# A two-layer transformer step on one core: the whole program ordered by the framework's timeline model

## The chip, the cores and the metric

The kernel runs on one core of a Trainium2 chip. Its time is device microseconds of one execution. The engines are TensorE (PE: matmuls, and PEld for their weight loads), VectorE (DVE), ScalarE (ACT), GpSimd (POOL) and SyncE (SP, which issues most of the loads). Each engine works through its own list of instructions in order and waits there for semaphores of the others.

## The reference

One inference step of a hybrid model, 1024 wide, for 128 context tokens and 512 latent tokens that go through the weights together. It has two layers, cut here to what the change touches:

```python
def trunk_layer(x, mods, gain1, gain2, w1, w2, mixer):
    shift1, scale1, gate1, shift2, scale2, gate2 = mods
    mix, aux = mixer(rms_norm(x, gain1) * (1 + scale1) + shift1)
    x = x + gate1 * mix
    h = rms_norm(x, gain2) * (1 + scale2) + shift2
    x = x + gate2 * (jnp.square(jax.nn.relu(h @ w1)) @ w2)
    return x, aux
```

`mods` is silu(c) times `w_mod`, 1024 by 6144 for each layer. The mixer of the first layer is softmax attention, with the keys and values of the context as further outputs. That of the second is a gated DeltaNet with eight heads: q, k, v and a gate z from a projection, a short convolution on q, k and v, and for each head a scan over chunks of 64 tokens in both directions. In a chunk a triangular matrix is inverted (`tinv`), and from chunk to chunk a 128x128 state is carried:

```python
v_new = u_i - w_i @ S
o = (q_i * jnp.exp(gc_i)[..., None]) @ S + qk_i @ v_new
S = S * jnp.exp(g_last)[..., None, None] + jnp.einsum('bhcd,bhce->bhde', k_i * ..., v_new)
```

The normalised and gated heads go through `w_out`. The final states are outputs too.

## The kernel before

Activations are held transposed, as 8 tiles of 128 features by 640 tokens. Each is split into a high and a low part, and each dense product is three products of such parts (`mm3`), 128x320 matmuls that follow each other. A weight block of 512 KB is loaded into one of three `raw` buffers by SP (L185), copied into its high part by ACT (L136) and subtracted to its low part by DVE or POOL (L133).

The program runs through the stages input and first norm (to about 48 us of the profile), attention (to 382), the first MLP (to 815), DeltaNet (to 1381) and the second MLP with the final norm.

Two things set the order of the work. The first is the order in which the code is written down. Where stages shall overlap, `weave` (L77) takes turns between generators, by weights. In `delta`, a round r weaves the projections and the convolution of head r (`dn_dense`), the decays of head r-1 (`dn_decay`), the inverse of head r-2 (`dn_inverse`) and the scan of head r-3 (`dn_scan`); rounds 6 and 7 also weave in the gates and outputs of heads 0 and 1 (`dn_z`, `dn_out`). Behind the rounds stands:

```python
        weave((self.dn_decay(n - 1), 20), (self.dn_inverse(n - 2), 4), (self.dn_scan(n - 3), 5))
        weave((self.dn_inverse(n - 1), 4), (self.dn_scan(n - 2), 5))
        drain(self.dn_scan(n - 1))
        ...
        weave((gated(left), 4 * len(left)), (mods(), MODW))
        self.first = self.prefetch(a["dn_w_out"][0], 0, [f * P for f in range(FT)])
        for i in range(DIRECT):
            self.load_act(i)
        drain(self.dn_out(n - 1))
```

`left` are the heads 2 to 7, and `mods()` computes two thirds of the second layer's `mods` (`modulate`, L362: 32x512 matmuls in four column strips of the array, 16 row blocks of `w_mod` in 32 loads). Heads 0 to 4 write their gated output to DRAM (`outd`, L1064) and `load_act` reloads it (L1123); heads 5 to 7 keep theirs.

The second is the framework's scheduler. It goes through the written program and gives each engine its list: where the next instruction in the written order isn't ready by its model of the machine, a later one that is ready may come first. So the z projections, which are written behind the last scan, already fill gaps of earlier scans in the order before. The scheduler's model is the default one of `tile.TileContext` (L1265).

A step of a scan (`step` in `dn_scan`, L994) is a chain: two matmuls with the state, `r` on DVE, a matmul `p1`, two copies on ACT, a matmul `p2` for the new state, which DVE adds up, and a matmul for the output. A scan has five pairs of steps, one of each direction, and a last pair for the context. The two states of a head are loaded by SP at its start (L1035).

Of the kernel before, what the change touches and what calls it, by code (L numbers as in the profile page):

```python
# [92 lines left out]
class Model:  # L93
# [76 lines left out]
            self.stt(y, t, 1.5, y, ALU.add, ALU.mult)  # L170
        return y

# [1 line left out]
    def raw(self, shape):  # L174
        return self.wp.tile(shape, F32, tag="raw", bufs=self.NRAW, name=self.nm("raw"))

# [46 lines left out]
    def prefetch(self, w, row0, cols):  # L223
        return [self.pair(w, row0, c) for c in cols[: self.NW // 2]]

# [1 line left out]
    def norm_acc(self, x, f, half):  # L227
        lo, hi = HALVES[half]
        if f == 0:
            acc = self.main("x", shape=[P, HALF])  # L230
            self.act(acc, x[f][:, lo:hi], AF.Square)
            self.sums[half] = [acc]
            return
        sq = self.half()
        self.act(sq, x[f][:, lo:hi], AF.Square)
        if f == FT - 1:
            self.sums[half].append(sq)
        else:
            acc = self.sums[half][0]
            self.tt(acc, acc, sq, ALU.add, self.nc.gpsimd)  # L240
# [66 lines left out]
                self.norm_acc(x, o, half)  # L307
        return sink

# [1 line left out]
    def setup(self):  # L311
        nc, a = self.nc, self.a
        self.ident = self.const([P, P])
# [147 lines left out]
            self.nc.sync.dma_start(out=x[f], in_=d[f])  # L461
        return x

# [1 line left out]
    def dec(self, dt=F32):  # L465
        return self.scr("dec", 3, [P, DEC], dt)

# [223 lines left out]
    def psum(self, name):  # L691
        return self.tc.tile_pool(name=name, bufs=1, space=bass.MemoryType.PSUM)

# [1 line left out]
    def mlp(self, l, h, x, first, mid):  # L695
        w1, w2 = self.a["mlp_w1"][l], self.a["mlp_w2"][l]
        NQ = DFF // D
        for q in range(NQ):
            acts = [(self.main("a", F32R), self.main("a", F32R)) for _ in range(FT)]

            def sink(o, half, ps):
                lo, hi = HALVES[half]
                r = self.half()
                self.act(r, ps, AF.Relu)
                t = self.half()
                self.stt(t, ps, 0.0, r, ALU.max, ALU.mult)
                self.split(t, acts[o][0][:, lo:hi], acts[o][1][:, lo:hi])

            yield from self.dense(w1, 0, [q * D + f * P for f in range(FT)], h, sink, first=first if q == 0 else None)
            yield from self.dense(w2, q * D, [f * P for f in range(FT)], acts, self.residual(x, l, 5, q == NQ - 1),  # L710
                                  last=GROUP if q == NQ - 1 else 1, mid=mid if q == NQ - 1 else None)

# [1 line left out]
    def vview(self, t, b, blk):  # L714
        base = t[:, 0, 0:1]
        pitch = list(base.ap[0])
        if blk is None:
            return bass.AP(base.tensor, base.offset, [pitch, [2 * b, T // (2 * b)], [T + b, 2], [1, b]])
        return bass.AP(base.tensor, base.offset + blk * P, [pitch, [2 * b, P // (2 * b)], [T + b, 2], [1, b]])
# [408 lines left out]
        self.acts[hd] = (self.main(tag, F32R), self.main(tag, F32R))  # L1128
        self.split(f, *self.acts[hd])

# [1 line left out]
    def run(self):  # L1132
        tc, nc, a = self.tc, self.nc, self.a
        pool = lambda name: tc.tile_pool(name=name, bufs=1)
# [134 lines left out]
```

## Time and profile before

| | us |
|---|---|
| median of 3 runs | 1922.67 |
| lowest and highest | 1917.06, 1923.22 |
| span of the profiled execution | 1910.3 |
| the median above that span | 12.4 |
| PE busy | 1800.1 (94%) |
| DVE busy | 1024.0 (54%) |
| ACT busy | 740.9 (39%) |
| POOL busy | 351.5 (18%) |

The profiled execution has its span as its own time; the runs of the table were timed apart from it. A line L146 is that of the helper for all matmuls and L133 and L139 are those of helpers on DVE, so groups are told apart by the tiles that they write and read. A weight or activation tile is named after its pool, as `scan`, `big`, `pd`, `blk`, `raw`. In the profile a matmul on fp32 data is two records, and one on the split parts one.

### The profile page before, as it was taken

To read this page: it belongs to the slowest core of one execution; us is meant where nothing else is said; L and a number is where in the kernel's file an instruction comes from. 1 tells how busy PE (TensorE), PEld (TensorE's weight loads), DVE (VectorE), ACT (ScalarE), POOL (GpSimd) and SP (SyncE) were. 2 spreads that over 40 slices of the span, in tenths; PEclk is the share of its full clock that TensorE was granted. 3 is DMA by queue.
4 is the path that set the end of the run, shared out by engine and by line. 5 is a ranking of instruction groups with operands and counts; after the bars stand their busy time and mean duration, and the time that the engine had idled before them with its cause. 6 is when DMAs were issued, how large, how long until landed. Compare 5 with 4: busy or idle time off the path is not lost.

```text
span 1910.3 us, 30501 instructions
## 1 busy us (share of the span) xinstructions
PE 1800.1 (94%) x11981; PEld 1667.6 (87%) x11981; DVE 1024.0 (54%) x2272; ACT 740.9 (39%) x1690; POOL 351.5 (18%) x379
## 2 busy tenths in 40 slices
PE   6998999999999999997899998899799999999998
PEld 2777877999999999997888888666799999999998
DVE  5546563534434434569888887744654434343442
ACT  2345542422313223356565546533433223131331
POOL 2343221300000000312333323321332000000002
PEclk9999999999999999998999999999898999999999
DMA  8641136245222222324122221456512222222211
GB/s 296 224 142 34 34 124 213 67 146 153 78 78 78 68 77 78 99 57 117 38 69 69 69 68 46 113 158 203 190 45 78 78 73 71 78 78 78 71 52 56
DMA packets 267669, 188.16 MB, mean 98 GB/s; under 512 B 40223, under 2 KB 242486, under 8 KB 267526
## 3 DMA queue, kind: packets, MB, share of 16 engines
q1 hardware_dynamic: 256032, 177.62, 31.7%
q10 hardware_dynamic: 10710, 6.83, 1.2%
q8 instruction: 94, 1.54, 0.3%
q0 software_dynamic: 784, 1.77, 0.2%
q14 instruction: 49, 0.40, 0.1%
HBM read 168.78 MB, written 14.79 MB: 96 GB/s over the span
## 4 chain that ended last, share of the span: by engine, by line
PE 75%; DVE 15%; DMA 5%; issue 2%; ACT 2%; POOL 0%; SPq 0%; ACTq 0%; POOLq 0%; DVEq 0%
PE dense L146 33%; PE pd L146 29%; PE scan L146 4%; DVE cv L139 2%; PE big L146 2%; PE mod L362 2%; PE pd L362 1%; DVE wide L133 1%; DMA wide<-gd 1%; DMA raw<-in_w_mod 1%; DVE w L133 1%; DVE ptmp L133 1%; DVE rst L133 1%; PE big L149 1%; PE S L146 1%
## 5 line engine op out<-in xcount | busy, mean ns | idle before, releaser
L146 PE MATMUL pd<-h,w 128*128 128x320 f32 x2016 | 358.7, 324 | 2.7 <-DVE a L133 2.4
L146 PE MATMUL dense<-a,wx 128*128 128x320 f32 x2238 | 337.0, 310 | 2.4 <-ACT wx L136 1.6
L146 PEld LDWEIGHTS dense<-a,wx 128*128 128x128 f32 x2238 | 329.7, 188 | 7.7 <-ACT wx L136 3.4
L146 PEld LDWEIGHTS pd<-h,w 128*128 128x128 f32 x2016 | 308.9, 194 | 15.7 <-issue 10.0
L136 ACT ACTIVATE wx<-raw 128x1024 fp32r<-128x1024 f32 x132 | 139.7, 1059 | 406.6 <-PE dense L146 220.6
L146 PE MATMUL dense<-h,wx 128*128 128x320 f32 x1776 | 265.1, 309 | 0.0
L146 PEld LDWEIGHTS dense<-h,wx 128*128 128x128 f32 x1776 | 261.6, 188 | 1.7 <-issue 1.7
L133 DVE TENSOR_TENSOR wx<-raw,wx 128x1024 fp32r<-128x1024 f32 x127 | 157.4, 1241 | 195.1 <-ACT wx L136 194.9
L133 POOL TENSOR_TENSOR x<-x,half 128x320 f32<-128x320 f32 x48 | 50.3, 1049 | 924.1 <-ACT half L136 889.8
L146 PE MATMUL pd<-a,wx 128*128 128x320 f32 x1284 | 194.3, 309 | 0.0
L146 PEld LDWEIGHTS pd<-a,wx 128*128 128x128 f32 x1284 | 189.6, 188 | 0.8 <-issue 0.8
L139 DVE SCALAR_TENSOR_TENSOR x<-dense,c,x 128x320 f32<-128x320 f32 (+2 forms) x152 | 61.8, 435 | 175.3 <-PE dense L146 175.2
L146 PE MATMUL pd<-h,wx 128*128 128x320 f32 x1008 | 151.8, 309 | 0.0
L146 PEld LDWEIGHTS pd<-h,wx 128*128 128x128 f32 x1008 | 148.8, 188 | 0.8 <-issue 0.8
L136 ACT ACTIVATE a<-half 128x320 fp32r<-128x320 f32 x128 | 60.1, 471 | 116.7 <-DVE half L139 116.7
L133 DVE TENSOR_TENSOR a<-half,a 128x320 fp32r<-128x320 f32 x128 | 62.8, 492 | 65.9 <-ACT a L136 65.6
L139 DVE SCALAR_TENSOR_TENSOR x<-pd,c,x 128x192 f32<-128x192 f32 (+2 forms) x88 | 36.0, 437 | 108.0 <-PE pd L146 108.0
L146 PE MATMUL scan<-blk,wide 128*128 128x128 f32 x288 | 64.9, 308 | 26.8 <-DVE blk L139 23.3
L146 PEld LDWEIGHTS scan<-blk,wide 128*128 128x128 f32 x288 | 44.6, 192 | 49.9 <-DVE blk L139 33.4
L139 DVE SCALAR_TENSOR_TENSOR cv<-cv,c,cv 128x644 f32<-128x644 f32 x84 | 84.3, 1004 | 2.0 <-ACT cv L136 0.9
L146 PE MATMUL big<-wide,a 128*128 128x128 f32 x480 | 71.9, 286 | 8.7 <-DVE wide L133 8.6
L136 ACT ACTIVATE w<-raw 128x1024 fp32r<-128x1024 f32 x54 | 57.0, 1060 | 45.4 <-PE pd L146 28.1
(276 smaller groups left out, 2529.9 us busy)
## 6 DMA issues: line engine op xcount, KB each, us to landing
raw<-in_mlp_w SPq DMA_DIRECT2D x128, 512.0 KB
raw<-in_w_mod SPq DMA_DIRECT2D x80, 512.0 KB
raw<-in_dn_w_in SPq DMA_DIRECT2D x32, 512.0 KB
raw<-in_attn_w_in SPq DMA_DIRECT2D x12, 512.0 KB
x<-xs SPq DMA_DIRECT2D x16, 320.0 KB
wide<-gd SPq DMA_DIRECT2D x16, 320.0 KB
h<-in_w_mod SPq DMA_DIRECT2D x16, 256.0 KB
a<-in_w_mod SPq DMA_DIRECT2D x16, 256.0 KB
```

What stands on the lines that cost most here:

```text
L133: (eng or self.nc.vector).tensor_tensor(out=out, in0=in0, in1=in1, op=op)
L136: self.nc.scalar.activation(out=out, in_=in_, func=func, **kw)
L139: self.nc.vector.scalar_tensor_tensor(out=out, in0=in0, scalar=s, in1=in1, op0=op0, op1=op1)
L146: self.nc.tensor.matmul(out, l, r, start=first, stop=last)
L149: self.nc.tensor.transpose(out, in_, self.ident[:n, :n])
L362: nc.tensor.matmul(ps[32 * q : 32 * q + 32, :], self.cond[:, k, :], views[q], start=k == 0, stop=k == FT - 1, tile_position=(0, 32 * q),)
```

## The change

It hands the scheduler another model of the machine, the framework's timeline model. Nothing else in the program changes; other lines of the diff remove comments.

```diff
-    with tile.TileContext(nc) as tc:
+    with tile.TileContext(nc, schedule_with_timeline_sim=True) as tc:
         body(tc, a, o)
```

The lists hold the same instructions, except that ACT loads its function tables five times fewer. Their order differs in most stages, most of all in the DeltaNet stage.

PE, at the first matmul of head 0's inverse (`big` from `wide`); the numbers in the names of the `pd` tiles grow in the order in which the program is written. Before:

```order
L146 MATMUL pd_1526_9100<-h_820_3768,w_1519_9054 128x320
L146 MATMUL pd_1526_9100<-h_821_3769,w_1519_9054 128x320
L146 MATMUL pd_1526_9100<-h_820_3768,w_1520_9055 128x320
L146 MATMUL big_1513_9028<-wide_1510_9020,a_1512_9026 128x128 x5
L146 MATMUL pd_1540_9175<-h_806_3754,w_1537_9170 128x320
```

Now:

```order
L146 MATMUL pd_1639_9657<-h_820_3768,w_1618_9575 128x320
L146 MATMUL pd_1639_9657<-h_821_3769,w_1618_9575 128x320
L146 MATMUL pd_1639_9657<-h_820_3768,w_1619_9576 128x320
L146 MATMUL big_1513_9028<-wide_1510_9020,a_1512_9026 128x128 x5
L146 MATMUL pd_1665_9762<-h_806_3754,w_1662_9757 128x320
```

The same inverse matmul now stands behind 144 more projection matmuls than before.

PE, in the scan of head 7 (`scan`), with z projections (`pd` from `h`) and `w_mod` matmuls (L362). Before:

```order
L146 MATMUL scan_2472_13253<-blk_2471_13250,wide_2261_12591 128x128
L149 MATMUL big_2544_13515<-c_6_82,a_1828_10565 128x128
L362 MATMUL pd_2548_13533<-raw_2563_13601,c_11_97 32x512 x2
L146 MATMUL pd_2564_13607<-h_814_3762,w_2555_13553 128x320
L146 MATMUL pd_2564_13607<-h_816_3764,w_2554_13552 128x320
L146 MATMUL pd_2564_13607<-h_817_3765,w_2554_13552 128x320
L146 MATMUL scan_2476_13264<-blk_2475_13262,wide_2397_13034 128x128
```

Now:

```order
L146 MATMUL scan_2472_13253<-blk_2471_13250,wide_2261_12591 128x128
L146 MATMUL scan_2476_13264<-blk_2475_13262,wide_2397_13034 128x128
L146 MATMUL scan_2479_13271<-blk_2477_13266,a_2254_12554 128x128
L146 MATMUL scan_2481_13277<-blk_2473_13255,x_2144_12037 128x128
L146 MATMUL scan_2481_13277<-blk_2473_13255,x_2198_12284 128x128
L146 MATMUL scan_2479_13271<-blk_2478_13268,wide_2261_12591 128x128
L149 MATMUL big_2575_13679<-c_6_82,a_1963_11178 128x128 x5
```

All projections and `w_mod` matmuls have moved ahead of the scans of heads 6 and 7; what is left between their steps are the last inverse and transposes (L149) of gated heads.

SP, around the loads of head 6's states (`blk_2364`, `blk_2365`). Before:

```order
L935 DMA td_2291_12724<-ptu_2290_12719 40x2x256
L937 DMA cm_2292_12727<-td_2291_12724 128x20x16
L1035 DMA blk_2364_12945<-in_state_delta 128x128
L1035 DMA blk_2365_12947<-in_state_delta 128x128
L390 DMA raw_2537_13479<-in_w_mod 128x1024
L390 DMA raw_2538_13485<-in_w_mod 128x1024
```

Now:

```order
L937 DMA cm_2292_12727<-td_2291_12724 128x20x16
L185 DMA raw_2693_14331<-in_dn_w_out 128x8x128
L185 DMA raw_2696_14337<-in_dn_w_out 128x8x128
L185 DMA raw_2699_14343<-in_dn_w_out 128x8x128
L1123 DMA x_2634_14052<-outd_8185 128x640
L1123 DMA x_2637_14058<-outd_8185 128x640
L1035 DMA blk_2364_12945<-in_state_delta 128x128
L1035 DMA blk_2365_12947<-in_state_delta 128x128
```

The `w_mod` loads have moved ahead of the state loads, and three loads of `dn_w_out` and two reloads now stand between them and the last decay's load.

## Rows read from the trace of the kernel before

**Rows 1.** The page's busy time, share of the span and instructions by engine.

```profile
span 1910.3 us, 30501 instructions
...
PE 1800.1 (94%) x11981; PEld 1667.6 (87%) x11981; DVE 1024.0 (54%) x2272; ACT 740.9 (39%) x1690; POOL 351.5 (18%) x379
```

**Rows 2.** Windows of the start and first MLP: length, busy times, clock, DMA share.

```profile
0.00:48.00 48.00, 30.70 (x139) 12.66 (x139) 27.24 (x57) 13.02 (x25) 13.66 (x25) 0.94 0.84 296
...
430.00:478.00 48.00, 48.00 (x329) 45.93 (x328) 19.65 (x33) 11.21 (x11) 0.00 (x0) 1.00 0.54 151
```

**Rows 3.** Chain that ended last, pieces in the first MLP: start, us, what.

```profile
436.56 1.00 PE mod L362 x8
...
441.26 7.06 PE pd L146 x48
```

**Rows 4.** Windows of the DeltaNet stage, same columns.

```profile
828.00:1200.00 372.00, 334.25 (x2324) 314.75 (x2322) 310.10 (x735) 216.97 (x626) 110.20 (x132) 0.95 0.26 64
1200.00:1264.00 64.00, 54.14 (x342) 38.49 (x341) 46.47 (x115) 29.46 (x89) 23.53 (x14) 0.95 0.50 144
1264.00:1334.00 70.00, 68.09 (x406) 44.63 (x405) 30.10 (x102) 27.29 (x95) 9.79 (x9) 1.00 0.57 176
1334.00:1381.00 47.00, 36.13 (x225) 34.23 (x224) 28.39 (x53) 21.42 (x55) 15.86 (x8) 0.92 0.56 176
```

**Rows 5.** Windows within the DeltaNet stage, same columns.

```profile
860.00:907.00 47.00, 35.31 (x216) 33.98 (x216) 43.92 (x105) 29.23 (x82) 13.27 (x21) 0.84 0.43 115
...
1098.00:1146.00 48.00, 45.06 (x329) 42.28 (x328) 39.11 (x104) 23.78 (x69) 12.47 (x15) 1.00 0.25 68
```

**Rows 6.** Waits from 828 to 1264: engine, line, waited for, us, times, longest.

```profile
PE scan L146 <- DVE blk L139: 23.3, 17, 2.6
...
PE big L146 <- DVE wide L133: 8.6, 2, 5.8
```

**Rows 7.** Chain that ended last, pieces of 1200 to 1385.

```profile
1212.67 5.28 DMA raw<-in_w_mod
...
1229.41 2.68 DMA ptmp<-gmd
...
1239.15 0.97 PE pd L362 x2
...
1242.66 1.00 PE pd L362 x8
...
1359.32 6.18 DMA x<-outd
...
1368.44 0.64 DVE a L133
...
1380.54 4.58 PE dense L146 x19
```

**Rows 8.** Chain that ended last, pieces of the start.

```profile
42.92 1.21 DVE w L133
```

**Rows 9.** Window of head 6's scan, instructions on scan tiles alone, same columns.

```profile
1259.00:1295.00 36.00, 15.93 (x88) 11.85 (x88) 8.44 (x27) 7.60 (x27) 1.00 0.52 167
```

**Rows 10.** Groups from 1259 to 1334: instruction, count, busy us, mean ns, idle before.

```profile
L146 PE MATMUL big<-wide,a 128*128 128x128 f32 x60 | 9.2, 278 | 0.0
...
L136 ACT ACTIVATE blk<-scan,cs 128x128 f32<-128x128 f32 x20 | 7.3, 367 | 21.7 <-PE scan L146 21.6
...
L139 DVE SCALAR_TENSOR_TENSOR blk<-scan,ng,a 128x128 f32<-128x128 f32 x16 | 5.6, 349 | 3.6 <-PE scan L146 2.9 <-PE big L149 0.2 <-ACT a L136 0.2
...
L149 PE MATMUL big<-c,a 128*128 128x128 f32 x25 | 4.0, 273 | 0.0
```

**Rows 11.** Group of the DeltaNet stage, 828 to 1381: VectorE's half of a weight split.

```profile
L133 DVE TENSOR_TENSOR w<-raw,w 128x1024 fp32r<-128x1024 f32 x32 | 42.7, 1336 | 10.9 <-ACT w L136 10.9
```

**Rows 12.** Windows of the two last scans, all instructions, same columns.

```profile
1259.00:1295.00 36.00, 34.57 (x212) 23.13 (x211) 14.32 (x35) 13.35 (x39) 9.88 (x6) 1.00 0.52 167
1296.00:1333.00 37.00, 35.49 (x201) 21.82 (x200) 18.11 (x71) 15.98 (x63) 4.91 (x5) 1.00 0.67 205
```

## The prediction

> **What bounds the kernel now.** I read the page's busy times first, then windows of the span, then the chain and the waits inside the worst windows. TensorE is busy 1800.1 of 1910.3 us, VectorE 1024.0 [rows 1]: only about 110 us are TensorE's idle time, and a new order can gain there or by making TensorE's own work cheaper, nowhere else. The windows show where idle is. In an MLP stage all 48.00 us of a window are busy with 329 matmuls, while the start has 30.70 of 48 [rows 2]; the MLP's chain pieces are runs of 128x320 matmuls, 48 in 7.06 us, so 0.147 us each [rows 3]. No order helps there. The DeltaNet stage, 828 to 1381, is the place: 334.25 of 372, 54.14 of 64, 68.09 of 70 and 36.13 of 47 us [rows 4], 492.6 of 553, so 60 us idle: 47.5 us up to 1264, where head 6's scan begins, 2 in the filled scans of heads 6 and 7, 11 behind them. Up to 1264 VectorE is nearly as full (310.10 of 372), and in 860 to 907 it is the bound, with 43.92 of 47 against TensorE's 35.31 [rows 5]. What TensorE waits for there is above all a scan's small VectorE result: 23.3 us in 17 waits [rows 6].
>
> **What the new order moves.** The instructions are the same (ACT has five table loads fewer, and ACT is nobody's bound). The MLP rows hardly move. In the DeltaNet stage the independent q/k/v and z projections run ahead: the first inverse matmul comes 144 projections later, and of the 240 that stood between the start of head 6's scan and the first dn_w_out projection none is left there. So the middle has more cover and the two last scans have none.
>
> **Work taken off TensorE.** The w_mod matmuls of the stage stand in 20 groups instead of 31. A group costs 0.97 us with 2 records and 1.00 us with 8 [rows 7], since the four that make one row block run beside each other; counting a group of five or six products as two units, 33 units become 24: 9 x 1.0 = 9 us less (between 0 and 11). In the first MLP, 11 groups become 15, and as that window has no idle, this costs 4 x 1.00 = 4 us [rows 2, 3]. At the start two stages of the first norm come sooner (a 128-column tile is finished before the next weight split, which takes 1.21 us [rows 8]): 1.5 us less, bounded by 0 and 3. Net of these two: +2.5 us.
>
> **Up to head 6's scan.** TensorE's work from there to the first dn_w_out projections that need all heads is two scans at 15.93 us each (head 6's [rows 9], and 44 matmuls in head 7's too), the last inverse 9.2 us and the transposes 4.0 us [rows 10], and 47 projections at 0.147: 31.9 + 13.2 + 6.9 = 52, with 1 for the last transposes 53 us. All the rest lies before: 492.6 - 9 - 53 = 430.6 us, so the scan starts at 828 + 430.6 + idle = 1258.6 + idle. The idle time was 47.5. For less: the projections put ahead cover the waits of rows 6 and the 12 us lost at 860 to 907. Against: VectorE has to do more splits sooner (32 of 1.34 us in the stage, eight or nine of them moved ahead [rows 11], 11 us), and the new order has three bursts of some 60 to 90 rows of scan and inverse with hardly a projection between them. Nothing in the trace gives that sum; its ends are 10 us (VectorE: 310.10 + 46.47 + 11 = 368 us of work [rows 4] ends long before) and 47.5. I take **36**: a third of the old waits go, the bursts keep the rest. Head 6's scan starts at 1294.6 (1268 to 1306).
>
> **The tail.** A step of a scan is two matmuls at about 0.28 us, a VectorE step 0.35, two matmuls, an ACT copy 0.37, two matmuls and a VectorE step 0.35 [rows 10]: 2.7 us in line, and two directions go side by side. A pair of steps holds 15.93 / 6 = 2.7 us of matmuls. So a pair takes 2.7 us if the directions overlap fully and 5.4 if not at all; I take 3.8, near the overlap, because each direction's vector steps are covered by the other's matmuls. Two scans of six pairs: 45.6 us; the inverse and the transposes fit into the gaps. On SP's queue the state loads of head 6 now stand behind three dn_w_out loads and two reloads, and each pair of state loads waits for the last matmuls of the scan before, with no projection left to cover it: a small load in this stage took 2.68 us [rows 7], twice 5.4. At the end comes the last head's norm and gate, some 12 us as now (from 1368.5 to 1380.54 [rows 7]); the last reload (6.18 us [rows 7]) lies beside it. The tail is 45.6 + 5.4 + 12 = **63 us**. Its ends: TensorE's 45 us of work and the 12, 57; and the pace of the filled scans, 36 and 37 us [rows 12], with the 12, 85.
>
> In SP's ring the two reloads (6.18 us each in the trace) stand ahead of the state load. The Trainium skill, DMA: Bandwidth & Descriptors, section Queues, rings and completion order, says that each DMA engine consumes descriptors in ring order. By that the load lands with the reload, 3.5 us later than taken, and the sum would be 1905.5.
>
> **The sum.** First dn_w_out rows with all heads: 1294.6 + 63 = 1357.6 instead of 1380.5, so -22.9; with +2.5, -20.4. The profiled execution has 1910.3 us of span, and the median 1922.67 lies 12.4 us above it; I keep that distance: 1922.67 - 20.4 = **1902**. A change below 0.3% (5.8 us) can't be told from none.
>
> **Rivals.** *The bare tail runs at the lower clock (slower).* In 860 to 907, with two waits for VectorE of 8.6 us in sum [rows 6], the granted clock was 0.84; in 1098 to 1146 it was 1.00 [rows 5]. The tail waits in every step. At the lower of its two levels (1.2 instead of 2.4 GHz) a pair has 5.4 us of matmuls, and 6.2 with 0.8 that does not overlap: 74.4 + 5.4 + 12 = 92 us; with some of it in the bursts too, idle 42: 1258.6 + 42 + 92 = 1392.6, +12 + 2.5, **1937**. It decides from 5.5 us per pair on: idle and tail may be 119.4 us together, and (119.4 - 36 - 17.4) / 12 = 5.5. For it: the pace with cover was 6 us. Against it: those 36 us were 34.57 us of matmuls, mostly of others [rows 12], and the gaps of a bare scan are short, where a wait of 860 to 907 lasted 5.8 us.
> The Trainium skill, TensorE: Matmul & The Clock Gate, section Why this matters for your kernels, says that idle gaps between bursts of matmuls throw TensorE back to half clock. By it the projections should have been kept for the tail, as now; the row of 860 to 907 agrees with the direction.
>
> *The w_mod loads become the wait (no change).* The 16 w_mod fetches (32 loads of 512 KB) and six z loads were spread from 1204 to 1325; now the w_mod part lies within some 87 us of TensorE's work. Three buffers and a load of 5.28 us [rows 7], one group and the issue make about 7.3 us per three: 38 loads need 92 us, and at the 205 GB/s of 1296 to 1333 [rows 12] 19.9 MB need 97. 10 us of that would be new stall, and as much again where VectorE's chain stands behind the loads on SP: +20, **1922**. Against it: the first 48 us moved 296 GB/s [rows 2].
>
> *The waits go altogether (more gain).* Idle 10 and a tail of 57: 1325.6, -55 + 2.5, **1870**. It needs VectorE never to be late, and it is 83% busy now.
>
> That the order stays as it was is out: the lists differ throughout the stage.
>
> **How the numbers follow.** Forecast 0.50, lower clock 0.27, loads 0.13, no waits 0.10. The forecast's own spread (1870 to 1936 by its bounds) puts 0.04 within 0.3%. Faster: 0.46 + 0.10 = 0.56. Same: 0.04 + 0.11 of the loads' case = 0.15. Slower: 0.27 + 0.02 = 0.29. The range goes from the case of no waits, 1870, to the lower clock with the old idle and more, 1944 (1937 + 7, the state loads behind the reloads on both scans).
>
> **What would show it.** Right: head 6's scan at 1285 to 1305; the two last scans in under 30 us each, with TensorE 60 to 80% busy and hardly a projection among them; the first MLP 4 us longer. Wrong: scans that still take 35 us (then look at the granted clock there first), waits for w_mod among the longest of TensorE, idle up to head 6's scan as large as before, or a gain in a stage whose order hardly moved.

## The result, and the profile after

The change takes **1997.7 us** (median of 4 runs, 1995.6 to 2002.7), the kernel before 1919.9 on the same chip: ratio **1.0418, 95% interval 1.0392 to 1.0443**. It is slower by 78 us, where 1902 us (1870 to 1944) was forecast. The page of the change, in the part that answers to [rows 1], with the slices of the clock:

```profile
span 1993.9 us, 30537 instructions
...
PE 1827.2 (92%) x11981; PEld 1694.4 (85%) x11981; DVE 1013.0 (51%) x2272; ACT 732.9 (37%) x1685; POOL 350.4 (18%) x379
...
PEclk8999999999999999998979989998589999999999
```

The matmuls are the same 11981, but TensorE is busy for 27 us more than in [rows 1], and the granted clock has its lowest slice, .5, at the 29th of 40. The spans of the two profiled executions lie 83.6 us apart; the rest of that, 56.5 us, is idle time of TensorE. Windows of the change (length, busy times, clock, DMA share, GB/s) show where: the first MLP, the DeltaNet stage up to head 6's scan, the scans of heads 6 and 7, and what is left to the first full dn_w_out projection.

```profile
437.00:485.00 48.00, 48.00 (x330) 45.93 (x330) 19.82 (x33) 11.09 (x11) 0.00 (x0) 1.00 0.51 147
833.00:1368.00 535.00, 456.85 (x2986) 407.39 (x2985) 368.34 (x877) 256.31 (x727) 126.48 (x150) 0.93 0.33 90
1368.00:1402.00 34.00, 27.65 (x158) 23.24 (x157) 10.53 (x30) 12.15 (x37) 7.94 (x6) 0.80 0.03 8
1402.00:1436.00 34.00, 27.07 (x110) 22.16 (x109) 17.82 (x79) 13.34 (x67) 6.74 (x7) 0.60 0.20 64
1436.00:1465.00 29.00, 11.66 (x53) 10.50 (x52) 19.68 (x36) 12.48 (x32) 13.42 (x6) 0.58 0.56 182
```

The same stretch of the kernel before, up to head 6's scan, is this window:

```profile
828.00:1259.00 431.00, 384.41 (x2644) 350.92 (x2641) 353.24 (x845) 244.30 (x705) 128.73 (x144) 0.95 0.29 74
```

The MLP is full as before ([rows 2]). The very first DeltaNet projection, still beside the MLP's last norm, is at 814.9 and 821.6. The milestones of the two traces, in us from the span's start (first instruction of a kind on TensorE), say that nearly everything is lost inside the DeltaNet stage:

| | before | change | later by |
|---|---|---|---|
| first projection of attention | 68.2 | 76.1 | 7.9 |
| first MLP begins | 409.3 | 416.6 | 7.3 |
| first DeltaNet projection behind the start of its gates | 835.1 | 839.6 | 4.5 |
| head 0's scan ends | 976.3 | 1049.3 | 73.0 |
| head 6's scan begins | 1259.4 | 1367.6 | 108.2 |
| head 7's scan ends | 1333.3 | 1436.1 | 102.8 |
| first full dn_w_out projection | 1380.5 | 1465.0 | 84.5 |
| second MLP begins | 1504.1 | 1585.7 | 81.6 |

In the stretch up to head 6's scan VectorE was busy for 353.24 of 431 us before and for 368.34 of 535 in the change. So its work stayed, and what it waits for grew. Its longest waits there in the change (what waited for what, us in total, times, longest us):

```profile
DVE blk L139 <- PE scan L146: 34.0, 19, 7.3
DVE a L133 <- PE scan L146: 26.9, 17, 6.2
DVE pn L143 <- DMA ptmp<-gmd: 18.6, 8, 4.0
DVE w L133 <- ACT w L136: 18.3, 9, 5.7
DVE cv L139 <- ACT cv L136: 12.6, 9, 3.3
DVE sse L143 <- ACT big L136: 12.3, 5, 5.7
```

The same view of the kernel before:

```profile
DVE blk L139 <- PE scan L146: 18.0, 22, 2.9
DVE a L133 <- PE scan L146: 14.9, 17, 3.7
DVE a L133 <- ACT gcol L136: 10.2, 1, 10.2
DVE pn L143 <- DMA ptmp<-gmd: 6.0, 2, 5.5
```

Before, the longest wait for a scan matmul was 3.7 us; in the change it is 7.3. For the halves of splits and convolutions that ScalarE hands over (w, cv) VectorE waited 1.1 us each before, and for the decay's DMA round trip through gmd 6.0 us in two waits; now it is 18.3, 12.6 and 18.6.

### The profile page after: what moved, and what is told of

It reads as the page before. It is cut to its first block, busy times and chain, and to the rows that moved or that the text cites. A ratio compares the mean times of both kernels' runs of the same rounds, so it can differ in the third digit from the quotient of the medians.

```text
span 1993.9 us, 30537 instructions
## 1 busy us (share of the span) xinstructions
PE 1827.2 (92%) x11981; PEld 1694.4 (85%) x11981; DVE 1013.0 (51%) x2272; ACT 732.9 (37%) x1685; POOL 350.4 (18%) x379
## 5 line engine op out<-in xcount | busy, mean ns | idle before, releaser
L146 PE MATMUL pd<-h,w 128*128 128x320 f32 x2016 | 339.1, 323 | 20.8 <-ACT cv L136 12.1
L146 PE MATMUL scan<-blk,wide 128*128 128x128 f32 x288 | 73.7, 345 | 31.4 <-DVE blk L139 10.6
L146 PEld LDWEIGHTS scan<-blk,wide 128*128 128x128 f32 x288 | 51.4, 220 | 54.5 <-DVE blk L139 20.9
L133 DVE TENSOR_TENSOR w<-raw,w 128x1024 fp32r<-128x1024 f32 x45 | 58.9, 1309 | 35.7 <-ACT w L136 35.4
```

The source lines that it names most:

```text
L133: (eng or self.nc.vector).tensor_tensor(out=out, in0=in0, in1=in1, op=op)
L146: self.nc.tensor.matmul(out, l, r, start=first, stop=last)
```

## The experiments

Most runs pin lists: once the whole program is written down, each instruction of an engine is tied to the one that shall stand ahead of it, and the model orders the rest. The core of the edit, the same for each engine:

```
+def pin(tc, nc, text):
...
+    for (n,) in struct.iter_unpack("<H", order):
+        i = traced["I-%d" % n]
+        if before is not None:
+            tc.add_manual_dep(i, before.name, free, reason="pin")
+        before = i
...
         body(tc, a, o)
+        pin(tc, nc, PE_ORDER)
```

The table puts the runs that pin or shift lists side by side; a run's ratio is to the kernel before as timed with it (medians of 1914.5 to 1919.9 us). "Head 6" is the start of its scan; the last four columns are VectorE's waits from 7 us ahead of the third row of the milestones to that point: all, for DMAs, for scan matmuls, for ScalarE. VectorE's busy time in that stretch is 342 to 369 us in every run, so length and waits go together by arithmetic; what a run tells is *which* wait came or went with its edit.

| run | us | ratio, 95% | head 6 | waits | DMA | scan | ScalarE |
|---|---|---|---|---|---|---|---|
| before | | 1 | 1259 | 66.6 | 10.7 | 33.1 | 13.0 |
| change | 1997.7 | 1.0418 (1.0392-1.0443) | 1368 | 155.2 | 29.9 | 66.8 | 44.4 |
| e1 TensorE's list of before | 1957.7 | 1.0194 (1.0160-1.0227) | 1308 | 110.2 | 41.2 | 39.7 | 18.3 |
| e5 TensorE's, VectorE's | 1923.9 | 1.0045 (1.0019-1.0071) | 1266 | 78.3 | 9.6 | 37.9 | 16.2 |
| e6 TensorE's, ScalarE's | 1945.6 | 1.0166 (1.0137-1.0195) | 1293 | 96.7 | 33.0 | 36.2 | 20.1 |
| e7 TensorE's, GpSimd's | 1957.1 | 1.0232 (1.0208-1.0256) | 1301 | 104.7 | 46.8 | 35.1 | 14.5 |
| e8 all four | 1912.0 | 0.9989 (0.9970-1.0008) | 1261 | 67.7 | 11.3 | 32.9 | 13.0 |
| e9 VectorE's alone | 2083.7 | 1.0868 (1.0842-1.0895) | 1432 | 225.5 | 8.5 | 179.7 | 12.2 |
| e12 before, TensorE's of the change | 2063.4 | 1.0773 (1.0745-1.0800) | 1427 | 194.9 | 22.5 | 89.7 | 53.2 |
| e15 VectorE's, ScalarE's, GpSimd's | 2027.3 | 1.0576 (1.0560-1.0593) | 1360 | 146.5 | 5.9 | 118.8 | 16.4 |
| e13 before, large pieces | 1954.5 | 1.0192 (1.0162-1.0223) | 1304 | 117.7 | 10.2 | 78.3 | 19.8 |
| e14 change, small pieces | 2005.1 | 1.0460 (1.0441-1.0479) | 1380 | 161.5 | 34.1 | 81.1 | 32.5 |

**Whose list is it?** e1 takes the change and pins TensorE's list to that of before.

> Timeline model, with TensorE's list pinned to the one of before; the other lists are left to the model. Theory A (the projections run ahead of the heads' chains on TensorE's list, so the chains are late and the last scans stand bare): within 10 us of before, 1912 to 1930. Theory C (the lists of VectorE, ScalarE and SyncE are what makes the chains late): at least 1950, as far as those lists stay those of the change.

It came out at 1957.7 us, in the range of theory C: TensorE's order, pinned first, is worth some 40 us, and as much is left, although the other lists now differ from before by 0.3 to 2 places in the mean. With it VectorE's waits for scan matmuls and for ScalarE come near those of before (58 in place of 111 us, before 46); those for DMAs do not (41.2, against 29.9 in the change). e5, e6, e7 and e8 pin a second list, or all but SP's queue:

```
         pin(tc, nc, PE_ORDER)
+        pin(tc, nc, DVE_ORDER)
```

> Timeline model, with the lists of TensorE and VectorE pinned to those of before; ScalarE, GpSimd and SyncE are left to the model. With TensorE's list alone pinned the time was 1957.7, 42 us over before, though the other lists had moved by only 0.3 to 2 rows on the mean. Theory C1 (VectorE's convolutions and weight splits now stand ahead of the small steps of scans and decays): most of the 42 us comes back, under 1930. Theories C2 (ScalarE's list) and C3 (GpSimd's list): 1945 or more.

> Timeline model, with the lists of TensorE and ScalarE pinned to those of before. Theory C2 (ScalarE's exponentials of the next decay now stand ahead of the evictions and copies that inverse and scan wait for): under 1930. Theories C1 and C3: 1945 or more.

> Timeline model, with the lists of TensorE and GpSimd pinned to those of before. Theory C3 (the pads of the convolution buffers, which wait for a free buffer, now stand ahead of GpSimd's part of the inverse and hold it up): under 1930. Theories C1 and C2: 1945 or more.

> Timeline model, with the lists of TensorE, VectorE, ScalarE and GpSimd pinned to those of before; only SyncE's loads are left to the model (0.3 rows moved on the mean, 11 at most). Theories C1 to C3: within 8 us of before, 1908 to 1925. Theory D (SyncE's order holds the loads of the chains back): 1940 or more.

Measured from e7, where GpSimd's list gave nothing, VectorE's list gives 33 us (1957.1 to 1923.9) and ScalarE's 11.5, and with all four the time is that of before. So the order of these four lists is the cause. SP's queue was left free in e8, but stays within 0.3 places of before in the mean, so the change's own order of loads is not tested by it. What VectorE's list changed stands in two answers on its waits. With TensorE's list alone (e1):

```profile
DVE pn L146 <- DMA ptmp<-gmd: 21.5, 8, 4.9
...
DVE wide L136 <- DMA cm<-td: 10.9, 7, 2.5
...
DVE gl L872 <- DMA wide<-gd: 8.8, 8, 2.4
```

With VectorE's too (e5; pinned kernels have line numbers higher by 3):

```profile
DVE pn L146 <- DMA ptmp<-gmd: 5.1, 1, 5.1
...
DVE gl L872 <- DMA wide<-gd: 3.1, 5, 1.1
```

The waits for DMAs fall from 41.2 to 9.6 us, by 31.6, and the time by 33. The new list puts steps that read back a small DMA where the data is still on its way, for the decay (pn) in all eight heads; under the old one a single such wait of 5.1 us is left.

**Are projections taken too early, or the w_mod matmuls?** e2, e3 and e4 leave the change as it is, but no z projection (e2), no q/k/v projection (e3), no w_mod matmul (e4) may stand ahead of the scan or inverse matmul behind which the kernel before has it:

```
+def hold(tc, nc, text):
...
+        if n < 0x8000:
+            last = i
+        elif last is not None:
+            tc.add_manual_dep(i, last.name, free, reason="hold")
```

> Timeline model, with the 288 z projections of heads 2 to 7 kept from standing earlier among the scans and inverses than they did before; the q/k/v projections and the w_mod matmuls stay free. VectorE's list moves by 1.4 rows on the mean from the changed one. Theory A: the scans of heads 0 to 3 stay as late as in the change (head 3's starts at 1165 to 1180), but the last two scans have cover again and the total falls to 1930 to 1960. Theory B (the w_mod loads are squeezed): hardly better, 1980 or more. Theory C (vector lists): 1975 or more.

> Timeline model, with the 1296 q/k/v projections (and z of heads 0 and 1) kept from standing earlier among the scans and inverses than before; z of heads 2 to 7 and w_mod stay free. Theory A: head 5's scan starts within 30 us of before's 1204 instead of 108 later; the last scan alone stays bare, total 1930 to 1960. Theory B: 1980 or more, as z and w_mod are still early.

> Timeline model, with only the 64 w_mod matmuls of slabs 1 and 2 kept from standing earlier among the scans and inverses than before. SP's queue then keeps the z weights back too, so 48, 44 and 76 z projections stand in the last three scans. Theory A: the last scans have cover, 1930 to 1960, as much as holding z back. Theory B: all of the loss comes back, under 1930, and TensorE's waits for w_mod (8.9 us in the change) go.

They took 1994.0 (ratio 1.0397), 1991.5 (1.0383) and 2001.7 us (1.0433). e2 and e3 lie in the ranges of their theories B; e4 lies in neither of its two. With z held, head 6's scan began at 1344 and head 7's ended at 1418 instead of 1436, but then z was still to do, and the first full dn_w_out projection came at 1463.7, against 1465.0 in the change. So keeping back one kind of projection gives 4 to 6 us of the 78 back, and that the projections are used up too soon is not the cause by itself (both kinds at once were held only together with the rest of TensorE's list, in e1). Nor are the w_mod matmuls and their loads, a rival of the prediction.

**Can a list be exchanged alone?** e9 pins VectorE's list only, e12 gives the kernel before (default model) TensorE's list of the change.

> Timeline model, with VectorE's list alone pinned to the one of before; TensorE and all others are left to the model. Theory E (the model puts long VectorE operations, convolutions and weight splits of 0.9 to 1.2 us, between the small dependent steps of the decays' recursion, 49 of them instead of 18, and so makes every head late): 1920 to 1940, with recursions of 105 us in sum over the eight heads as before (154 in the change). Theory P (TensorE's list is the larger part by itself): 1960 or more.

> Default model, with TensorE's list pinned to the one of the change; the other lists are left to the default model, which then puts 28 long operations into the recursions. Theory P: 1985 or more, as slow as the change. Theory E: 1940 to 1970, as far as the recursions are shorter than in the change (115 to 130 us in sum); what is over before in spite of that is the part of TensorE's own list, the two bare scans at the end.

Both are slower than either whole: 2083.7 and 2063.4 us, in the ranges of theory P; theory E of e9 was off by over 140 us. Some instructions of e9 in order of time (start, us, engine, line, what, count; in brackets idle time and what ended it):

```profile
1198.40 0.61 PE L149 MATMUL scan<-blk,x 128*128 128x128 f32 x4
...
1198.77 3.77 PE L149 MATMUL pd<-h,w 128*128 128x320 f32 x24
...
1202.37 0.39 PE L149 MATMUL scan<-blk,wide 128*128 128x128 f32 x2
...
1202.51 2.46 PE L149 MATMUL pd<-h,w 128*128 128x320 f32 x15
...
1206.22 0.38 PE L149 MATMUL scan<-blk,a 128*128 128x128 f32 x2
...
1206.64 0.35 DVE L142 SCALAR_TENSOR_TENSOR blk<-blk,ex,scan 128x128 f32<-128x128 f32 x1 [7.04 <-PE scan L149]
```

Between two steps of a scan TensorE works off 24 and then 15 projections in a row, and VectorE, whose list goes on with the scan's result, stands still for 7.04 us. In the kernel before the pieces are short: in heads 1 to 4 its 631 projections between scan steps come in 101 pieces, in the change 542 matmuls in 48, here 638 in 42 (w_mod matmuls, some 60 in the change, are counted with the projections). e15 pins the three vector lists and leaves TensorE's to the model (656 in 42 pieces).

> The new model, with the lists of VectorE, ScalarE and GpSimd of the kernel before; TensorE's is left to the model, which puts 656 projections between the scan steps of heads 1 to 4 in 42 pieces, most of 18 to 29 matmuls (the run with VectorE's list alone, 2083.7 us, had 638 in 42). Theory A, TensorE's pieces beside vector lists that are made for small ones are what cost there: 2000 us or more, VectorE's waits for scan matmuls over 100 us. Theory B, ScalarE's list of the new model beside VectorE's of before cost there: 1940 us or less.

2027.3 us, with 118.8 us of waits for scan matmuls: theory A. TensorE's list beside vector lists made for small pieces costs 111 us against before, of which 77 lie between the third milestone and head 6's scan (502 us, in the change 528); the rest is lost ahead of it and behind. The other 56 us of e9 went with ScalarE's and GpSimd's lists of before, so theory B has a part in it.

**The size of the pieces by itself.** e13 has all four lists of before, as e8, and only the places of TensorE's projections in heads 1 to 4 are shifted into pieces of 24. e14 has the change's TensorE list with pieces of at most about six there.

```
+        pin(tc, nc, PE_ORDER)
+        pin(tc, nc, DVE_ORDER)
+        pin(tc, nc, ACT_ORDER)
+        pin(tc, nc, POOL_ORDER)
```

> The lists of VectorE, ScalarE and GpSimd are those of the kernel before, and TensorE's too, but for one thing: between the scan steps of heads 1 to 4, where the kernel before puts its projections in 101 pieces (631 matmuls, 6.2 in the mean), they stand in 27 pieces of 24, each taken ahead of its old place. The change has 48 pieces, 11.3 in the mean. Theory A, pieces: a scan step that is ready behind 24 projections waits up to 24 x 0.147 = 3.5 us, and what waits for it on VectorE and ScalarE waits too. Over 27 pieces in place of 101, about 27 x 1 us or more: 1930 to 1955 us, VectorE's waits for scan matmuls up from 33 us to 55 or more. Theory B, the chain has room for that: 1912 to 1922 us, VectorE's waits as before.

> The change, with TensorE's list as it has it, but in heads 1 to 4 no piece of projections between two scan steps holds more than about 6 matmuls: 48 pieces become 90 (the same 542 matmuls, each at its old place or later). The other lists are left to the new model and move by less than a row in the mean. Theory A, pieces: the steps come earlier, scans 1 to 4 are 5 to 8 us shorter each: 1965 to 1980 us. Theory B, the waits of the vector engines for other things (the DMA round trip ahead of the recursion, ScalarE's halves of splits and convolutions) are what holds the chain: 1990 to 2000 us.

e13 took 1954.5 us, 38.4 more than before, with the same instructions and vector lists. VectorE's waits there:

```profile
DVE blk L142 <- PE scan L149: 53.9, 28, 5.8
DVE a L136 <- PE scan L149: 24.2, 23, 3.7
```

That is 78.3 us for scan matmuls in place of 33.1, and head 6's scan begins 45 us later. Large pieces alone can cost half of what the change lost. They are twice as large as the change's own (11.3 in the mean), so the run doesn't say how much of the change's loss is theirs. And e14 is a miss, outside both theories: 2005.1 us, 7 more than the change. Small pieces beside vector lists that were made for large ones give nothing back; waits for scan matmuls went up to 81.1 us. Then e18 asked whether still smaller pieces help the kernel before (122 pieces, none above six; with it the five dn_w_out splits on VectorE):

> The kernel before, default model, with two edits: TensorE's list has in heads 1 to 4 no piece of projections between two scan steps above about 6 matmuls (122 pieces in place of 101, the same 631 matmuls, at their old place or later; the vector lists are left to the model), and the five splits of dn_w_out weights are on VectorE in place of GpSimd. Theory A, smaller pieces help further: scans 1 to 4 end 5 to 10 us earlier in sum, and the last norm is 2 to 5 us shorter: 1900 to 1912 us, ratio 0.992 to 0.998. Theory B, with 6.2 matmuls in the mean the chain is no longer held by pieces, and what is left is other waits: 1912 to 1922 us.

1914.8 us, ratio 1.0008 (0.9992 to 1.0024): theory B. Below the 6.2 projections in the mean of before, smaller pieces give nothing, and no version found is faster than the kernel before beyond its interval.

**Long operations in the decay's recursion.** Between the 32 dependent steps of each head's recursion the new list puts, over all heads, 49 long operations of about 1 us, most of them convolutions and weight splits (before: 18). e10 keeps them behind the recursion in the change, e11 in the kernel before.

```
+def after_recursions(tc, nc, pairs):
...
+    for i, last in pairs:
+        tc.add_manual_dep(traced["I-%d" % i], "I-%d" % last, free, reason="after recursion")
```

> Timeline model, nothing pinned, but the convolutions and weight splits that stood inside a recursion of VectorE have to stand behind its last step; 17 long operations (sums, products and splits for other heads) are left inside instead of 49. Theory E: recursions of 115 to 125 us in sum instead of 154, the last scan ends 25 to 40 us earlier, total 1955 to 1972. Theory P: 1985 or more, though the recursions are shorter.

> Default model, with the same rule: convolutions and splits kept out of the recursions; 8 long operations inside instead of 18. Theory E: the recursions take 92 to 98 us in sum instead of 104, and the total falls below before by 3 to 10 us (1904 to 1911 against 1914). If the recursion is not on the path that sets the end there: within 3 us of before.

The eight recursions of the change took 153.8 us in sum, with e10 120.9 (before: 104.3), yet the time was 1996.8 us (1.0416); e11 gave 1916.4 (0.9993). A striking row, but shortening it gave no time in either kernel.

**The tail.** From head 6's scan on the change needs 97.4 us. e17 moves head 6's multiplication by its norm from GpSimd, where TensorE waits 12.6 us for it, to VectorE. e16 fills the steps of the last two scans with matmuls that nobody reads (this is added work), and puts the five dn_w_out splits on VectorE.

```
-        eng = nc.gpsimd if hd < HEADS - 1 else nc.vector
+        eng = nc.gpsimd if hd < HEADS - 2 else nc.vector
```

> The change with one instruction moved: head 6's multiplication by its norm is on VectorE in place of GpSimd, where it stood behind three splits of weights for the second MLP. All other lists are the change's, row by row. In the trace of the change TensorE waits 12.6 us for it ahead of the last transposes. Theory A, that wait is on the path that sets the end: 1985 to 1992 us, and from the last scan's end to the first full dn_w_out projection 17 to 21 us in place of 29. Theory B, the last head's own norm comes as late: 1994 us or more.

```
             self.mm(p2[:, P : 2 * P], dm[:, d, s], y)
+            for _ in range(WARM if hd >= HEADS - 2 else 0):
+                self.mm(p2[:, 2 * P : 3 * P], dm[:, d, s], y)
...
-            drain(self.dense(a["dn_w_out"][0], 0, FC, acts, self.residual(x, 1, 2), first=self.first, last=GROUP, mid=mid3, eng=nc.gpsimd))
+            drain(self.dense(a["dn_w_out"][0], 0, FC, acts, self.residual(x, 1, 2), first=self.first, last=GROUP, mid=mid3))
```

> The change with two edits that touch its tail alone; up to head 6's scan all lists are the change's. (1) In each of the 20 steps of the last two scans the matmul of dm with y is done four more times, into columns that nobody reads (added work: 80 fp32 matmuls, which fill gaps). (2) The five splits of dn_w_out weights that stand on GpSimd beside the last heads' norms are on VectorE; in the change small VectorE steps of 128x5 elements take 2.3 us there, 0.17 elsewhere. Theory A for (1): the clock of .50 to .70 is most of why a bare scan took 34 us: the granted clock rises to 0.9 or more and a scan takes 26 to 31 us. Theory B: the steps of the two directions stand one behind the other, and the clock is their consequence: 34 us or more. Theory A for (2): the slow VectorE steps hold the tail: from the last scan's end to the first full dn_w_out projection 18 to 22 us in place of 29. Theory B: the splits take as long on VectorE itself: 27 us or more. Both A: 1970 to 1985 us; both B: 1994 to 2010.

e17: 1997.4 us, no gain. VectorE and GpSimd at the end of its last scan:

```profile
1438.26 9.84 POOL L133 TENSOR_TENSOR wx<-raw,wx 128x1024 fp32r<-128x1024 f32 x4 [4.05 <-ACT wx L136]
...
1441.24 2.28 DVE L143 TENSOR_SCALAR sso<-sso 128x5 f32<-128x5 f32 x1
1443.56 2.27 DVE L139 SCALAR_TENSOR_TENSOR sso<-ssc,sso 128x5 f32<-128x5 f32 x1
1445.86 2.27 DVE L143 TENSOR_SCALAR rsy<-sso 128x5 int32<-128x5 int32 x1
1448.16 0.17 DVE L133 TENSOR_TENSOR rst<-rsy 128x5 f32<-128x5 f32 x1
```

The wait for GpSimd has become one of 16.5 us for VectorE, where steps of 128x5 elements take 2.3 us beside GpSimd's splits; the three in a row here make 6.8 us of it. e16 took 1996.4 us. Its windows of the same two scans:

```profile
1368.00:1402.00 34.00, 30.33 (x212) 27.77 (x213) 10.63 (x29) 10.45 (x30) 8.81 (x6) 0.89 0.01 3
1402.00:1436.00 34.00, 27.03 (x188) 23.53 (x186) 17.82 (x76) 13.55 (x69) 5.49 (x6) 0.95 0.17 56
```

The clock rose from .80 and .60 to .89 and .95, but the two scans took 71.7 us, against 68.5 in the change: in each step the four added matmuls (eight records of about 0.14 us) stand in line with it and used up whatever the clock gave. The time is that of theory B, the clock that of theory A, so the run does not price the clock cleanly. Two other runs come nearer: over the first eight steps of head 7's scan ScalarE's copies lie 3.0 us apart in e15 (4 projections among them, clock .92) and 3.1 in e2 (21 projections, .98), against 3.5 in the change (none, .64). That makes some 0.5 us per step for the clock, 1 us per pair of steps; the vector lists differ between these runs, so it is an estimate. With the splits on VectorE the 2.3 us steps are gone, but the splits wait there for ScalarE's halves, in the middle of the norm, and TensorE waited 12.9 us, against 12.6 in the change.

## Why the prediction was wrong

**The bound: the step that failed.** Up to head 6's scan the prediction counted TensorE's work and added idle time between 10 us, since VectorE's 368 us of work "ends long before", and the old 47.5; it chose 36. VectorE's work was 368.34 us, as counted. But a list that is worked off in order also waits, and VectorE's waits are 155.2 us in place of 66.6. So the stretch took 535 us and not 466.6: TensorE's idle time is 78, not 36 (42 more), its matmuls took 456.85 us, not 430.6 (26 more; the granted clock was .93, against .95 in the window of before, and no run says how much of the 26 is the clock's), and the stage began some 5 us later. That is the 73 us between 1294.6 and 1367.6. The old idle time was no upper end: it was what the old order left, and a new one can leave more.

What made the waits is shown in two parts. TensorE's list makes 53 of them (scans and ScalarE, change against e1); that large pieces of projections between scan steps can make such waits by themselves is shown in the order of before (e13). VectorE's list makes those for small DMAs: 32 us beside TensorE's list of before (e1 against e5); in the change itself they are 29.9, 19 over before. Which property of the lists would give the time back inside the change stays open: small pieces, held projections and undisturbed recursions each returned little or nothing, and e9, e12 and e15 say why one property is hard to take out, as each list is made for the others.

**Cover in the middle.** The projections put ahead do cover the waits that the prediction named: up to head 0's scan those for VectorE's inverse steps fall from 8.6 us ([rows 6]) to 1.0. But a new wait takes their place, for the halves of convolutions from ScalarE. Over the stretch up to head 6's scan:

```profile
PE pd L146 <- ACT cv L136: 12.1, 8, 3.7
```

Of these, 10.6 us lie ahead of head 0's scan, and TensorE's idle time up to there is 17.7 us in place of 14.5. The other 28 us of added idle time come behind its beginning, where VectorE's waits for scan matmuls are.

**The tail: mis-sized.** Forecast 63 us, measured 97.4: scans of 34.5 and 34.0 us in place of two of 22.8 and loads of 5.4, and 28.9 in place of 12 for the norm. A pair of steps was taken as 3.8 us, "near the overlap", and a scan as six pairs. It has five, the context's among them: [rows 10] have 20 copies to `blk` with `cs`, one for each step, in two scans. So a pair took 6.9 us, above even the 5.4 without overlap, and with five pairs the forecast's own terms would have been 7.6 us shorter. The two directions stand one behind the other in TensorE's list. The 5.4 us for state loads were nothing: in these two scans TensorE never waits for one. The rival with the lower clock had the tail nearly right (92 us) by luck: with six pairs its scans came to 74.4 us, where 68.5 were measured, and its norm to 12. It had the granted clock (.80, then .60, both means over its two levels, against 1.00 in [rows 12]), but by the estimate from e15 and e2 the clock makes 1 us of the 3.1 that a pair took too long, and at .92 a pair still took 6.0. Its idle time of 42 us was nearly as far off as the forecast's.

The rule that it leaned on, that idle gaps throw TensorE back to half clock (the Trainium skill, TensorE: Matmul & The Clock Gate, section Why this matters for your kernels), agrees with these rows in its direction; the longest of TensorE's waits in head 7's scan is 1.1 us. The norm's 17 us too much were not in any case: weight splits on GpSimd for the next stage lie beside it, and neither e16 nor e17, which move a part of that work, got them back.

**What held, and the small terms that did not.** The w_mod groups held: 37.3 us of matmuls before, 27.9 after, 9.4 less where 9 was said. The small terms ahead of the DeltaNet stage were +2.5 in sum and came out as +4.5, but neither for its reason: the 1.5 us to be saved at the first norm came out on the other side (the first projection is 7.9 us later), and the 4 us for w_mod in the first MLP are not there, which has four groups of them in both traces. The distance of median and span was 12.4 us in the forecast and is 3.8 here, which hides 8.6 us of the miss.

## What to carry to other kernels

Where two engines are each busy for over 80% of a stage, count for both what they wait for in their own order, not only what they work: the second engine's in-order waits can be the larger term, and the old idle time bounds nothing from above. Between dependent small steps, large pieces of filler can cost what the other engine cannot bridge (shown in the order of before, e13), and a step that reads back a DMA wants other work ahead of it. Lists of different engines that come from one plan shouldn't be judged or exchanged one by one: of the mixtures with one plan's TensorE list and the other's VectorE list, e1, e6 and e7, with TensorE's of before, lie between the two wholes, and e9, e12 and e15, with TensorE's from the new model, are slower than both.

## What was unexpected on the chip

In e17 a VectorE instruction of 128x5 elements takes 0.17 us, but 2.3 us while GpSimd works on splits of 128x1024 (9.84 us for four, so 2.46 each): VectorE gets through about one small step per GpSimd instruction. The Trainium skill, SBUF — State Buffer, section Summary: rules for kernel authors, says that of VectorE and GpSimd the second to issue blocks fully until the first is done, where VectorE reads two inputs or runs in its two-port mode; the rows of e17 agree in what they take, but steps with a single input tensor are among the slow ones, and no row shows the mode that they ran in. In e16, with the splits elsewhere, all these steps took 0.16 or 0.17 us.
